# Turning the retention's q and k without TensorE: VectorE squares and transfers, with the row norms broadcast through DRAM and the forget sums made transposed

## The chip, the cores and the metric

The kernel runs on one core of a Trainium2 chip. The metric is device microseconds from launch to end. A core has five engines that matter here, each with its own queue that is worked off in order: TensorE (PE, matrix products), VectorE (DVE), ScalarE (ACT), GpSimd (POOL), and SyncE (SP), which issues nearly all transfers. An instruction that waits holds up everything behind it on its own engine.

## The reference

One decoder block on 512 tokens of width 1024, in float32. Two token mixers run side by side, a chunkwise retention and an attention with forget gates; then come gates, an output projection and a SwiGLU feed-forward part. What the change touches:

```python
q_r = rotary(q_r.reshape(B, S, RET_HEADS, RET_DK), pos)                          # 4 heads of 64
k_r = rotary(k_r.reshape(B, S, RET_HEADS, RET_DK), pos) * (RET_DK ** -0.5)
# retention, chunks of 128 tokens:
scores = jnp.einsum('bnihd,bnjhd->bnhij', qc, kc) * decay[None, None]
intra = jnp.einsum('bnhij,bnjhe->bnihe', scores, vc)
chunk_kv = jnp.einsum('bnjhd,hj,bnjhe->bnhde', kc, zeta, vc)
inter = jnp.einsum('bnihd,bnhde->bnihe', qc, states) * xi[None, None, :, :, None]
# forgetting attention:
log_f = jax.nn.log_sigmoid(f_f.astype(jnp.float32) + b_forget[l].astype(jnp.float32))
c = jnp.cumsum(log_f, axis=1).transpose(0, 2, 1)
s = s + c_blk[..., None] - c[:, :, None, :]
```

`RMSNorm(x)` scales each token by one number (the row norm); the kernel applies it after the product, so for the gates, which are computed with tokens along the free axis, that number must stand in every partition: a [128, 512] tile `r1`.

## The kernel before

Every large product is made in three parts (high x high, low x high, high x low) to keep float32 accuracy. So each weight tile `raw` of 512 KB is loaded by SP, cast by ACT to `wh` (L162) and has its remainder `wl` made by VectorE (L163). There are two `raw` buffers and three pairs of `wh`/`wl`: a load waits until the tile before last has been split, a cast until TensorE is done with the weights three units back.

The stretch in question runs from about 60 to 175 us. TensorE's order there is written out by hand: a generator `fill` yields the weight products of the other projections (for the attention `qf` with 256 and then 264 columns, `kf`, `vf`, and then the gates), and `fill(us)` puts so many microseconds of them between the steps of the retention. The steps work on one chunk t of 128 tokens, t = 0 to 3: `ret_rotate` (POOL, rotary embedding, writes `rot` and the keys `kz`), `ret_turn` (TensorE turns `rot` in four 128 x 128 transposes against an identity, ACT copies them out of a `tp` bank into `rT`, VectorE multiplies the q half by a decay), `ret_scores` (two `tp` banks, products of `rT`, then `kz` x `vr` for the state), `ret_values` (two `sc` banks), `ret_norm` (VectorE, group norm into `og`) and `ret_out` (VectorE gates `og`, TensorE turns it, ACT and VectorE split it into `orh` and `orl`). There are two `tp` banks, so the scores of chunk t+1 need `ret_out` of t-1 to have left its bank: `orl` (L189) is what frees it.

Meanwhile the finished `qf` is squared by ACT, summed and normalized by VectorE (the `n8` instructions, interleaved with the `n4` of the retention's norm) and multiplied by POOL (L642, L644), and then turned through VectorE squares and DRAM (`turn_heads`, `put_heads`, `get_heads`). All transfers after 60 us go through `move` (L72) on SP's one queue, in the order of the program. The function `after(a, b)` only fixes the order of two instructions.

`broadcast_cols` makes `r1`: VectorE spreads the four columns of row norms into `wide`, TensorE turns it (four transposes), ACT copies it out. The forget sums are made as [tokens, heads] by two small products, copied to `cs`, turned by four transposes, and put to DRAM as `cd`.

Of the kernel before, what the change touches and what calls it, by code (L numbers as in the profile page):

```python
# [9 lines left out]
F32 = mybir.dt.float32  # L10
# [42 lines left out]
def block_kernel(ctx: ExitStack, tc, x, xT, c_early, c_tab, c_late, w_qf, w_tok, w_vg, w_a, w_y, w_o, w_gu, w_gl, w_dn, w_dh, out):  # L53
# [198 lines left out]
    ri = sm.tile([P, 32], F32, name="ri", tag="ri", bufs=1)  # L252
    nc.gpsimd.memset(ri, 0.0)

    def broadcast_cols(r, dst, wide=None, behind=None):

        pb = bank("tp")
        if wide is not None:
            one = nc.vector.tensor_copy(out=wide, in_=r.rearrange("p (t o) -> p t o", o=1).broadcast_to([P, NT, P]))
            if behind is not None:  # L260
                after(one, behind)
        for t in range(NT):
            if wide is None:
                rb = sm.tile([P, P], F32, name="rb", tag="rb")
                ts(out=rb, in0=ones, scalar1=r[:, t:t + 1], scalar2=None, op0=ALU.mult)
            turn(pb[:, t * P:(t + 1) * P], rb if wide is None else wide[:, t, :])
        nc.scalar.copy(out=dst, in_=pb)
# [196 lines left out]
    s4 = x_low(0)  # L464
    b6.append(half(B22, 1))
    products(z_, b6, s4, False)
    wide = ftok.tile([P, NT, P], F32, name="wide", tag="sq", bufs=1)
    vr = rtok.tile([P, NT, 512], F32, name="vr", tag="rtok0")
    gs = rtok.tile([P, NT, 512], F32, name="gs", tag="rtok1")
    for v in range(2):  # L470
# [49 lines left out]
    def ret_rotate(t):  # L520
        z5 = rz[:, t, :].rearrange("p (a h s d) -> p a h s d", a=2, h=RH, s=2)
        z1, z2 = z5[:, :, :, 0, :], z5[:, :, :, 1, :]
        c = cosv[:, t].broadcast_to([P, 2, RH, 32])
        s = sinv[:, t].broadcast_to([P, 2, RH, 32])
        rot = rwk.tile([P, 512], F32, name="rot", tag="rot")
        r5 = rot.rearrange("p (a h s d) -> p a h s d", a=2, h=RH, s=2)
        ta = rwk.tile([P, 2, RH, 32], F32, name="ta", tag="ta", bufs=1)
        tb = rwk.tile([P, 2, RH, 32], F32, name="tb", tag="tb", bufs=1)
        first = gp.tensor_tensor(out=ta, in0=z1, in1=c, op=ALU.mult)
        if t == 0:  # L530
            tc.add_manual_dep(first.ins, last_low.ins.name, mybir.DependencyInfo(mybir.DependencyClass.Sync, mybir.DependencyReason.DATA), reason="GpSimd's part comes behind most of the sums")
# [6 lines left out]
        gp.tensor_tensor(out=r5[:, :, :, 1, :], in0=tcc, in1=td, op=ALU.add)
        kz = rwk.tile([P, 256], F32, name="kz", tag="kz")
        last = gp.tensor_tensor(out=kz.rearrange("p (h d) -> p h d", h=RH), in0=rot[:, 256:512].rearrange("p (h d) -> p h d", h=RH),  # L540
                         in1=ce[:, C_ZETA:C_ZETA + RH].rearrange("p (h o) -> p h o", o=1).broadcast_to([P, RH, RDK]), op=ALU.mult)
        ret[t].update(rot=rot, kz=kz, rotated=last)

    def ret_turn(t):
        rot = ret[t]["rot"]
        rT = rwk.tile([P, 6, P], F32, name="rT", tag="rT")
        pt = bank("tp")
        for j in range(4):
            turn(pt[:, j * P:(j + 1) * P], rot[:, j * P:(j + 1) * P])
        nc.scalar.copy(out=rT[:, 0:4, :], in_=pt.rearrange("p (j q) -> p j q", j=4))  # L550
        tt(out=rT[:, 4:6, :], in0=rT[:, 0:2, :], in1=xiT, op=ALU.mult)
        ret[t].update(rT=rT)

    def ret_scores(t):
        rT, kz = ret[t]["rT"], ret[t]["kz"]
        sT = rwk.tile([P, 512], F32, name="sT", tag="sT")
        sps = [bank("tp") for e in range(2)]
        for e, sp in enumerate(sps):
            rows = slice(e * 64, (e + 1) * 64)
            for a in range(2):  # L560
                mm(sp[:, a * P:(a + 1) * P], lhsT=rT[rows, 2 + a, :], rhs=rT[rows, a, :], start=True, stop=True)
            tt(out=sT[:, e * 256:(e + 1) * 256], in0=sp[:, 0:256], in1=dec[:, e * 256:(e + 1) * 256], op=ALU.mult)  # L562
        ret[t].update(sT=sT)
        if t < NT - 1:
            kv = (ret[t - 1]["o"][0] if t else bank("sc"))[:, 256:512]
            for h in range(RH):
                rows = slice((h % 2) * 64, (h % 2 + 1) * 64)
                mm(kv[rows, (h // 2) * P:(h // 2 + 1) * P], lhsT=kz[:, h * RDK:(h + 1) * RDK], rhs=vr[:, t, h * P:(h + 1) * P], start=True, stop=True)
            sn = rwk.tile([P, 2, P], F32, name="sn", tag="sn")
            if t == 0:  # L570
                nc.vector.tensor_copy(out=sn, in_=kv.rearrange("p (a e) -> p a e", a=2))
            else:
                st = ret[t]["st"]
                for a in range(2):
                    stt(out=sn[:, a, :], in0=st[:, a, :], scalar=ce[:, C_GCH + a:C_GCH + a + 1], in1=kv[:, a * P:(a + 1) * P], op0=ALU.mult, op1=ALU.add)
            ret[t + 1].update(st=sn)

    def ret_values(t):
        rT, sT = ret[t]["rT"], ret[t]["sT"]
# [28 lines left out]

    def ret_out(t):
        og = ret[t]["og"]  # L610
        after(gp.tensor_tensor(out=gs[:, t, :], in0=gs[:, t, :], in1=gret, op=ALU.mult), ret[1]["rotated"])
        tt(out=og, in0=og, in1=gs[:, t, :], op=ALU.mult)
# [58 lines left out]
    def turn_heads(z, ts_=range(NT)):  # L671
# [1 line left out]
        if 0 in ts_:  # L673
            turn_heads.sq = rtok.tile([P, 4, 4, NT, 32], F32, name="zsq", tag="rz")
        for t in ts_:
            nc.vector.transpose(out=turn_heads.sq.rearrange("p b a t j -> p a b t j")[:, :, :, t, :], in_=z[:, t, :].rearrange("p (a b j) -> p a b j", a=4, b=4))
# [212 lines left out]
    stt(out=lff, in0=fzf, scalar=0.0, in1=fa, op0=ALU.min, op1=ALU.subtract)
    lp = ftok.tile([P, NT - 1, FH], F32, name="lp")  # L890
    nc.vector.tensor_copy(out=lp[:, 0, :], in_=lf[:, 0, :])
    for j in range(1, NT - 1):
        tt(out=lp[:, j, :], in0=lp[:, j - 1, :], in1=lf[:, j, :], op=ALU.add)
# [12 lines left out]
    pc = bank("tp")
    for t in range(NT):
        turn(pc[0:FH, t * P:(t + 1) * P], cs[:, t, :])
    cT = ftok.tile([FH, S], F32, name="cT", tag="sq", bufs=1)
    nc.vector.tensor_scalar_mul(cT, pc[0:FH, :], -1.0)  # L910
    cd = drp.tile([FH, S], F32, name="cd")
    move(cd, cT)
# [647 lines left out]
```

## Time and profile before

| | |
|---|---|
| median of 3 runs | 683.05 us (683.03 to 683.46) |
| the profiled execution | 682.73 us, its span 680.9 us (1.8 us lie around the span) |
| TensorE busy | 673.2 us, 99% of the span |
| VectorE, ScalarE, GpSimd busy | 535.5, 351.0, 76.2 us |
| granted TensorE clock | 0.999 of full speed |

The profile names engines PE, DVE, ACT, POOL, SP; "PEld" is TensorE's weight load, "SPq" SP's issuing of transfers. A row `tp<-ctab,rot` is an instruction that writes tile `tp` and reads `ctab` (the identity lies in it) and `rot`. Matrix products overlap in the pipeline, so the start of one against the start of the next gives its cost, not its duration. A group in a timeline row ("x4") has one start and one length.

### The profile page before, as it was taken

How to read it: one execution, taken by the hardware profiler on the slowest of the kernel's cores; microseconds unless marked ns; L12 is line 12 of the kernel's file. 1: busy time of each engine (PE TensorE's matmuls, PEld its weight loads, DVE VectorE, ACT ScalarE, POOL GpSimd, SP SyncE). 2: the span in 40 equal slices, each digit the busy share in tenths (PEclk: the TensorE clock that was granted, in tenths of full speed). 3: DMA queues.
4: the chain of work that ended last, by engine and by line, in shares of the span. 5: the costliest groups of instructions: out<-in, count | busy, mean ns of one | idle time of the engine just before them, and what ended most of it. 6: DMA issues, size and time to landing. Idle time of an engine off the chain costs nothing.

```text
span 680.9 us, 9401 instructions
## 1 busy us (share of the span) xinstructions
PE 673.2 (99%) x3399; PEld 564.3 (83%) x3399; DVE 535.5 (79%) x865; ACT 351.0 (52%) x516; POOL 76.2 (11%) x96
## 2 busy tenths in 40 slices
PE   8999999999999999999999999999999999999998
PEld 6888997888886778788888888888888898888998
DVE  6899567777688674596989998989999888556794
ACT  6767452433464445254576655564646474343341
POOL 0013945101122210000130000000000000000000
PEclk9999999999999999999999999999999999999999
DMA  8910312624657886337511516445362513554221
GB/s 277 420 53 32 125 63 61 218 86 163 202 169 217 268 270 208 107 111 278 216 63 49 199 32 191 114 145 153 88 179 59 154 63 81 143 145 159 93 94 63
DMA packets 82223, 98.94 MB, mean 145 GB/s; under 512 B 52472, under 2 KB 59256, under 8 KB 81408
## 3 DMA queue, kind: packets, MB, share of 16 engines
q1 hardware_dynamic: 81392, 97.27, 44.8%
q10 hardware_dynamic: 784, 1.06, 0.6%
q8 instruction: 27, 0.44, 0.3%
q14 instruction: 20, 0.16, 0.1%
HBM read 81.97 MB, written 9.52 MB: 134 GB/s over the span
## 4 chain that ended last, share of the span: by engine, by line
PE 79%; DVE 1%; DMA 1%; issue 1%; ACT 1%; SPq 0%; DVEq 0%; ACTq 0%
PE acc L82 62%; PE sc L82 12%; PE tp L82 5%; DMA pT<-pd 1%; ACT ps L1058 0%; DVE ps L1059 0%; PE tp L85 0%; SPq L72 0%; DVE b L1067 0%; DVE wl L163 0%; DVE psq L751 0%; ACT us L1221 0%; DVE us L1271 0%; DVE orl L189 0%; DVE hl L1115 0%
## 5 line engine op out<-in xcount | busy, mean ns | idle before, releaser
L82 PE MATMUL acc<-ps,xfh 128*128 128x512 f32 (+1 forms) x576 | 166.6, 372 | 0.3 <-ACT us L1180 0.3
L82 PEld LDWEIGHTS acc<-ps,xfh 128*128 128x128 f32 x576 | 105.2, 188 | 19.1 <-ACT us L1180 0.5
L1058 ACT CAST ps<-b 128x1024 fp32r<-128x1024 f32 (+1 forms) x84 | 82.4, 981 | 59.9 <-DVE b L1067 26.7
L1059 DVE TENSOR_TENSOR ps<-b,ps 128x1024 fp32r<-128x1024 f32 (+1 forms) x84 | 94.3, 1135 | 20.1 <-ACT ps L1058 18.9
L82 PE MATMUL acc<-ps,xfl 128*128 128x512 f32 (+1 forms) x288 | 106.9, 371 | 0.0
L162 ACT CAST wh<-raw 128x1024 fp32r<-128x1024 f32 (+1 forms) x44 | 46.0, 1049 | 84.1 <-PE acc L82 42.2
L163 DVE TENSOR_TENSOR wl<-raw,wh 128x1024 fp32r<-128x1024 f32 (+1 forms) x44 | 56.5, 1288 | 24.0 <-ACT wh L162 24.0
L82 PEld LDWEIGHTS acc<-ps,xfl 128*128 128x128 f32 x288 | 54.3, 188 | 9.4
L1067 DVE TENSOR_TENSOR b<-b,b 128x1024 f32<-128x1024 f32 (+1 forms) x48 | 52.1, 1125 | 0.0
L82 PE MATMUL acc<-xh,wh 128*128 128x512 f32 x128 | 50.8, 397 | 0.0
L82 PE MATMUL acc<-wh,xh 128*128 128x512 f32 (+2 forms) x144 | 50.3, 350 | 0.0
L82 PE MATMUL acc<-xl,wh 128*128 128x512 f32 x128 | 50.0, 390 | 0.0
L82 PE MATMUL acc<-xh,wl 128*128 128x512 f32 x128 | 49.9, 390 | 0.0
L82 PE MATMUL acc<-wh,xl 128*128 128x512 f32 (+2 forms) x144 | 49.3, 343 | 0.0
L82 PE MATMUL acc<-wl,xh 128*128 128x512 f32 (+2 forms) x144 | 49.3, 342 | 0.0
L82 PE MATMUL acc<-hl,ps 128*128 128x512 f32 x168 | 40.4, 389 | 0.0
L82 PEld LDWEIGHTS acc<-hl,ps 128*128 128x128 f32 x168 | 31.5, 188 | 6.6
L1180 ACT COPY us<-acc 128x512 f32<-128x512 f32 (+1 forms) x48 | 26.1, 550 | 16.3 <-PE acc L82 15.3
L1106 DVE TENSOR_TENSOR ps<-raw,ps 128x1024 fp32r<-128x1024 f32 x14 | 17.1, 1220 | 18.8 <-ACT ps L1103 18.8
L82 PEld LDWEIGHTS acc<-wh,xh 128*128 128x128 f32 x144 | 27.2, 189 | 3.6 <-DVE sT L562 0.2
L82 PEld LDWEIGHTS acc<-wh,xl 128*128 128x128 f32 x144 | 27.2, 189 | 3.2
L82 PEld LDWEIGHTS acc<-wl,xh 128*128 128x128 f32 x144 | 27.2, 189 | 2.9
(302 smaller groups left out, 1438.8 us busy)
## 6 DMA issues: line engine op xcount, KB each, us to landing
b<-in_w_gu_dram SPq DMA_DIRECT2D x40, 512.0 KB, 4.2
raw<-in_w_a_dram SPq DMA_DIRECT2D x16, 512.0 KB, 4.5
raw<-in_w_dn_dram SPq DMA_DIRECT2D x14, 512.0 KB, 4.0
pd<-psq SPq DMA_DIRECT2D x8, 640.0 KB, 4.5
pT<-pd SPq DMA_DIRECT2D x32, 160.0 KB, 4.5
pf<-squares SPq DMA_DIRECT2D x160, 32.0 KB, 1.9
blk<-in_w_vg_dram SPq DMA_DIRECT2D x8, 512.0 KB, 10.0
raw<-in_w_tok_dram SPq DMA_DIRECT2D x8, 512.0 KB, 3.2
```

Source lines behind the costliest of these rows:

```text
L82: in_order(nc.tensor.matmul(o, **kw))
L162: split_raw.last = (nc.scalar.copy(out=h[:, :width], in_=raw[:, :width]), tt(out=l[:, :width], in0=raw[:, :width], in1=f32(h)[:, :width], ...
L163: tt(out=l[:, :width], in0=raw[:, :width], in1=f32(h)[:, :width], op=ALU.subtract))
L1058: part.cast = nc.scalar.copy(out=h, in_=raw)
L1059: low = tt(out=l, in0=raw, in1=f32(h), op=ALU.subtract)
L1067: queue(tt(out=raws[g][b][v], in0=raws[g][b][v], in1=raws[g][c][v], op=ALU.add))
L1106: tt(out=l, in0=raw, in1=f32(h), op=ALU.subtract)
L1180: copy = nc.scalar.copy(out=u_(tp, slot), in_=os[tp][:, :w])
```

## The change

It has four parts.

- Each chunk's `rot` is turned by one VectorE instruction in 32 x 32 squares (`ret_square`), put to DRAM in four transfers of 64 KB that set the squares in place, and got back as `rT` in one of 256 KB (`ret_get`). ACT copies the k half to `rK` (`ret_keys`), VectorE multiplies the q half into `rX` (`ret_decay`). The 16 transposes and the copies out of `tp` go. `rot` and `kz` get a third buffer, and the rotations are issued one chunk earlier.
- `put_cols` puts the row norms to DRAM, [1, 512], and one transfer reads them back into all partitions as `r1`. The spreading copy, four transposes and a copy go.
- The forget sums are made as [heads, tokens] at once: the log gates are the stationary operand and the triangle and ones move. Four transposes and a copy go.
- Orders: the first step of the log gates (`fa`) and VectorE's turning of `qf` come behind `og` of chunk 0.

```diff
-    def broadcast_cols(r, dst, wide=None, behind=None):
...
+    def put_cols(r, dst):
+
+        move(dst.rearrange("o (t p) -> p (o t)", p=P), r)
...
-    def ret_turn(t):
-        rot = ret[t]["rot"]
-        rT = rwk.tile([P, 6, P], F32, name="rT", tag="rT")
-        pt = bank("tp")
-        for j in range(4):
-            turn(pt[:, j * P:(j + 1) * P], rot[:, j * P:(j + 1) * P])
-        nc.scalar.copy(out=rT[:, 0:4, :], in_=pt.rearrange("p (j q) -> p j q", j=4))
-        tt(out=rT[:, 4:6, :], in0=rT[:, 0:2, :], in1=xiT, op=ALU.mult)
+    def ret_square(t):
+        sq = rwk.tile([P, 4, 4, 32], F32, name="rsq", tag="rsq")
+        one = nc.vector.transpose(out=sq.rearrange("p b a i -> p a b i"), in_=ret[t]["rot"].rearrange("p (a b j) -> p a b j", a=4, b=4))
+        after(one, (turn_of[0], ret[0].get("decay"), ret[1].get("new"), ret[2].get("new"))[t])
+        zd = drp.tile([4, 32, 4, P], F32, name="zr", tag=f"zr{t % 2}")
+        for c in range(4):
+            move(zd[:, :, c, :].rearrange("b j x -> j b x"), sq[32 * c:32 * c + 32].rearrange("p b a i -> p b (a i)"))
+        ret[t].update(zd=zd)
+
+    def ret_get(t):
+        rT = rwk.tile([P, 4, 4, 32], F32, name="rT", tag="rT")
+        move(rT.rearrange("p c a i -> p (c a i)"), ret[t]["zd"].rearrange("b j c x -> (b j) (c x)"))
...
     ret_rotate(0)
+    ret_rotate(1)
+    ret_square(0)
     fill(RF[0])
-    broadcast_cols(rstd1, r1, wide, turn_of[0])
-    ret_turn(0)
-    ret_rotate(1)
+    rd1 = drp.tile([1, S], F32, name="rd1")
+    put_cols(rstd1, rd1)
+    ret_get(0)
+    ret_rotate(2)
     fill(RF[1])
+    move(r1, rd1.broadcast_to([P, S]))
+    ret_keys(0)
     ret_scores(0)
+    ret_decay(0)
+    ret_square(1)
     for t in range(NT):
+        if t == 1:
+            ret_rotate(t + 2)
         fill(RF[2])
         if t + 1 < NT:
-            ret_turn(t + 1)
-            if t + 2 < NT:
-                ret_rotate(t + 2)
+            ret_get(t + 1)
         if t:
             fill(RF[3])
             ret_out(t - 1)
         turn_q()
         fill(RF[3])
+        if t + 2 < NT:
+            ret_square(t + 2)
         turn_q()
+        if t + 1 < NT:
+            ret_decay(t + 1)
+            ret_keys(t + 1)
         ret_values(t)
...
-    mm(cps[:, :NT * FH], lhsT=tri, rhs=lff, start=True, stop=False)
+    mm(cps[rows, :P], lhsT=lf.rearrange("p h t -> p (h t)"), rhs=tri, start=True, stop=False)
```

In the built program SP's queue changes most, where the first weight tiles of this stretch are loaded. `zr` is the DRAM tile of the squares, `rsq` the squares, `r_88` is `r1`:

```order
-L72 DMA raw<-in_w_qf_dram 128x1056 x2
-L72 DMA raw<-in_w_tok_dram 128x1024 x7
+L72 DMA raw<-in_w_qf_dram 128x1056
+L72 DMA zr<-rsq 32x4x128 x4
+L72 DMA raw<-in_w_qf_dram 128x1056
+L72 DMA rd_754<-rstd_86 128x4x1
+L72 DMA rT<-zr 128x512
+L72 DMA r_88<-rd_754 128x512
+L72 DMA zr<-rsq 32x4x128 x4
+L72 DMA raw<-in_w_tok_dram 128x1024 x2
+L72 DMA rT<-zr 128x512
+L72 DMA zr<-rsq 32x4x128 x4
```

Puts and gets of the squares now stand between the weight loads; the first two `w_tok` tiles stand behind the squares of chunk 1.

On VectorE, between the group norm's statistics of chunk 0 (`bs`, `mv`) and the reciprocal roots of the two norms, there now stand the squares of chunk 3 and the decay of chunk 2:

```order
+L604 BN_AGGR mv<-bs 128x2
+L534 STREAM_TRANSPOSE rsq<-rot 128x4x4x32
+L124 TENSOR_SCALAR n8v<-s_651 128x32
 L124 TENSOR_SCALAR n4v<-mv 128x4
+L553 TENSOR_TENSOR rX<-rT,cl 128x256
 L127 TENSOR_SCALAR n8y<-n8v 128x32
```

The two new instructions have come ahead of everything that ends in `og` of chunk 0.

Still on VectorE, in the midst of those roots:

```order
 L132 SCALAR_TENSOR_TENSOR n8y<-n8a,n8y 128x32
 L132 SCALAR_TENSOR_TENSOR n4y<-n4a,n4y 128x4
+L163 TENSOR_TENSOR wl<-raw,wh 128x1024
 L130 SCALAR_TENSOR_TENSOR n8a<-n8y 128x32
 L130 SCALAR_TENSOR_TENSOR n4a<-n4y 128x4
```

One weight remainder has come ahead of `og` of chunk 0; before, it stood behind the turning of `qf`.

And at the end of that chain on VectorE, around `og` itself:

```order
-L606 TENSOR_SCALAR og<-sc,mv,r_1026 128x128 x4
-L551 TENSOR_TENSOR rT<-rT,cl 128x256
-L612 TENSOR_TENSOR og<-og,gs 128x512
-L676 STREAM_TRANSPOSE zsq<-qf 128x4x4x32 x4
-L163 TENSOR_TENSOR wl<-raw,wh 128x1024
+L132 SCALAR_TENSOR_TENSOR r_979<-n8a,n8y 128x32
+L132 SCALAR_TENSOR_TENSOR r_1038<-n4a,n4y 128x4
+L609 TENSOR_SCALAR og<-sc,mv,r_1038 128x128 x4
+L615 TENSOR_TENSOR og<-og,gs 128x512
+L679 STREAM_TRANSPOSE zsq<-qf 128x4x4x32 x3
 L189 TENSOR_TENSOR orl<-tp,orh 128x4x128
```

The decay (`rT`) is gone from between the two `og` instructions, and `orl` comes ahead of the last square and of the remainder.

More of the change, by code (lines that the diff above doesn't have):

```diff
@@ L253, in block_kernel @@
     nc.gpsimd.memset(ri, 0.0)
-    def broadcast_cols(r, dst, wide=None, behind=None):
[L257 to L267, printed above, removed]
+    def put_cols(r, dst):
+        move(dst.rearrange("o (t p) -> p (o t)", p=P), r)
     def tok_group(src, evac, cuts=(512,), done=(), behind=None):
@@ L466, in block_kernel @@
     products(z_, b6, s4, False)
-    wide = ftok.tile([P, NT, P], F32, name="wide", tag="sq", bufs=1)
     vr = rtok.tile([P, NT, 512], F32, name="vr", tag="rtok0")
@@ L524, in ret_rotate @@
         s = sinv[:, t].broadcast_to([P, 2, RH, 32])
-        rot = rwk.tile([P, 512], F32, name="rot", tag="rot")
+        rot = rwk.tile([P, 512], F32, name="rot", tag="rot", bufs=3)
         r5 = rot.rearrange("p (a h s d) -> p a h s d", a=2, h=RH, s=2)
@@ L538, in ret_rotate @@
         gp.tensor_tensor(out=r5[:, :, :, 1, :], in0=tcc, in1=td, op=ALU.add)
-        kz = rwk.tile([P, 256], F32, name="kz", tag="kz")
+        kz = rwk.tile([P, 256], F32, name="kz", tag="kz", bufs=3)
         last = gp.tensor_tensor(out=kz.rearrange("p (h d) -> p h d", h=RH), in0=rot[:, 256:512].rearrange("p (h d) -> p h d", h=RH),
@@ L542, in ret_rotate, with ret_keys, ret_decay @@
         ret[t].update(rot=rot, kz=kz, rotated=last)
-    def ret_turn(t):
-        rot = ret[t]["rot"]
-        rT = rwk.tile([P, 6, P], F32, name="rT", tag="rT")
-        pt = bank("tp")
-        for j in range(4):
-            turn(pt[:, j * P:(j + 1) * P], rot[:, j * P:(j + 1) * P])
-        nc.scalar.copy(out=rT[:, 0:4, :], in_=pt.rearrange("p (j q) -> p j q", j=4))
-        tt(out=rT[:, 4:6, :], in0=rT[:, 0:2, :], in1=xiT, op=ALU.mult)
-        ret[t].update(rT=rT)
+    def ret_square(t):
[9 more added lines that the diff above has]
+        move(rT.rearrange("p c a i -> p (c a i)"), ret[t]["zd"].rearrange("b j c x -> (b j) (c x)"))
+        ret[t].update(rT=rT)
+    def ret_keys(t):
+        rK = rwk.tile([P, 2, P], F32, name="rK", tag="rK")
+        nc.scalar.copy(out=rK.rearrange("p a (c i) -> p a c i", i=32), in_=ret[t]["rT"][:, :, 2:4, :].rearrange("p c a i -> p a c i"))
+        ret[t].update(rK=rK)
+    def ret_decay(t):
+        rX = rwk.tile([P, 2, P], F32, name="rX", tag="rX")
+        ret[t]["decay"] = tt(out=rX.rearrange("p a (c i) -> p a c i", i=32), in0=ret[t]["rT"][:, :, 0:2, :].rearrange("p c a i -> p a c i"),
+           in1=xiT.rearrange("p a (c i) -> p a c i", i=32), op=ALU.mult)
+        ret[t].update(rX=rX)
     def ret_scores(t):
@@ L560, in ret_scores @@
             for a in range(2):
-                mm(sp[:, a * P:(a + 1) * P], lhsT=rT[rows, 2 + a, :], rhs=rT[rows, a, :], start=True, stop=True)
+                mm(sp[:, a * P:(a + 1) * P], lhsT=ret[t]["rK"][rows, a, :], rhs=rT[rows, :, a, :], start=True, stop=True)
             tt(out=sT[:, e * 256:(e + 1) * 256], in0=sp[:, 0:256], in1=dec[:, e * 256:(e + 1) * 256], op=ALU.mult)
@@ L570, in ret_scores @@
             if t == 0:
-                nc.vector.tensor_copy(out=sn, in_=kv.rearrange("p (a e) -> p a e", a=2))
+                new = nc.vector.tensor_copy(out=sn, in_=kv.rearrange("p (a e) -> p a e", a=2))
             else:
@@ L574, in ret_scores @@
                 for a in range(2):
-                    stt(out=sn[:, a, :], in0=st[:, a, :], scalar=ce[:, C_GCH + a:C_GCH + a + 1], in1=kv[:, a * P:(a + 1) * P], op0=ALU.mult, op1=ALU.add)
-            ret[t + 1].update(st=sn)
+                    new = stt(out=sn[:, a, :], in0=st[:, a, :], scalar=ce[:, C_GCH + a:C_GCH + a + 1], in1=kv[:, a * P:(a + 1) * P], op0=ALU.mult, op1=ALU.add)
+            ret[t + 1].update(st=sn, new=new)
     def ret_values(t):
@@ L587, in ret_values @@
                 rows = slice(e * 64, (e + 1) * 64)
-                mm(o[e][:, os], lhsT=rT[rows, 4 + a, :], rhs=ret[t]["st"][rows, a, :], start=False, stop=True, skip_group_check=True)
+                mm(o[e][:, os], lhsT=ret[t]["rX"][rows, a, :], rhs=ret[t]["st"][rows, a, :], start=False, stop=True, skip_group_check=True)
         ret[t].update(o=o)
@@ L610, in ret_out @@
         og = ret[t]["og"]
-        after(gp.tensor_tensor(out=gs[:, t, :], in0=gs[:, t, :], in1=gret, op=ALU.mult), ret[1]["rotated"])
-        tt(out=og, in0=og, in1=gs[:, t, :], op=ALU.mult)
+        after(gp.tensor_tensor(out=gs[:, t, :], in0=gs[:, t, :], in1=gret, op=ALU.mult), ret[2]["rotated"])
+        ret[t]["out"] = tt(out=og, in0=og, in1=gs[:, t, :], op=ALU.mult)
         pt = bank("tp")
@@ L675, in turn_heads @@
         for t in ts_:
-            nc.vector.transpose(out=turn_heads.sq.rearrange("p b a t j -> p a b t j")[:, :, :, t, :], in_=z[:, t, :].rearrange("p (a b j) -> p a b j", a=4, b=4))
+            one = nc.vector.transpose(out=turn_heads.sq.rearrange("p b a t j -> p a b t j")[:, :, :, t, :], in_=z[:, t, :].rearrange("p (a b j) -> p a b j", a=4, b=4))
+            if "out" in ret[0]:
+                after(one, ret[0]["out"])
     def put_heads(z, sq, name):
@@ L883, in block_kernel @@
     fa = ftok.tile([P, NT * FH], F32, name="fa")
-    lf = ftok.tile([P, NT, FH], F32, name="lf")
-    lff = lf.rearrange("p t h -> p (t h)")
-    stt(out=fa, in0=fzf, scalar=-1.0, in1=fzf, op0=ALU.mult, op1=ALU.max)
+    lf = ftok.tile([P, FH, NT], F32, name="lf")
+    lp = ftok.tile([P, FH, NT], F32, name="lp")
+    gp.memset(lp, 0.0)
+    one = stt(out=fa, in0=fzf, scalar=-1.0, in1=fzf, op0=ALU.mult, op1=ALU.max)
+    after(one, ret[0]["out"])
     act(out=fa, in_=fa, func=AF.Exp, scale=-1.0)
     act(out=fa, in_=fa, func=AF.Ln, bias=1.0)
[L889 to L893, printed above, removed]
+    stt(out=lf.rearrange("p h t -> p t h"), in0=fz, scalar=0.0, in1=fa.rearrange("p (t h) -> p t h", t=NT), op0=ALU.min, op1=ALU.subtract)
+    for j in range(NT - 1):
+        tt(out=lp[:, :, j + 1], in0=lp[:, :, j], in1=lf[:, :, j], op=ALU.add)
     put_heads(kf, turn_heads.sq, "k")
@@ L896, in block_kernel @@
     cps = bank("tp")
-    mm(cps[:, :NT * FH], lhsT=tri, rhs=lff, start=True, stop=False)
-    mm(cps[:, FH:NT * FH], lhsT=ones, rhs=lp.rearrange("p t h -> p (t h)"), start=False, stop=True)
-    cs = ftok.tile([P, NT, FH], F32, name="cs")
+    rows = slice(0, FH * NT)
+    mm(cps[rows, :P], lhsT=lf.rearrange("p h t -> p (h t)"), rhs=tri, start=True, stop=False)
+    mm(cps[rows, :P], lhsT=lp.rearrange("p h t -> p (h t)"), rhs=ones, start=False, stop=True)
     ftok.tile([P, PAD_FTOK], F32, name="pad")
-    nc.vector.tensor_copy(out=cs, in_=cps[:, 0:NT * FH].rearrange("p (t h) -> p t h", t=NT))
+    cT = ftok.tile([FH * NT, P], F32, name="cT", tag="sq", bufs=1)
+    nc.vector.tensor_scalar_mul(cT, cps[rows, :P], -1.0)
     get_heads(kf)
@@ L904, in block_kernel @@
     rtok.release()
+    cd = drp.tile([FH, S], F32, name="cd")
+    move(cd.rearrange("h (t q) -> (h t) q", t=NT), cT)
     fill(CF[1])
[L906 to L912, printed above, removed]
     ofp = tc.alloc_tile_pool(name="ofp", bufs=1, side="right")
```

## The prediction

> **What bounds the kernel now.** I read the table of engines first, then TensorE's waits, then the chain that ended last.
>
> ```profile
> PE 673.2 (99%) x3399; PEld 564.3 (83%) x3399; DVE 535.5 (79%) x865; ACT 351.0 (52%) x516; POOL 76.2 (11%) x96
> ```
>
> ```profile
> PE tp L82 <- DVE orl L189: 0.6, 1, 0.6
> ```
>
> ```profile
> 113.74 0.61 DVE orl L189
> ...
> 114.39 0.71 PE tp L82 x4
> ...
> 134.08 0.54 PE tp L82 x8
> ...
> 168.85 0.36 PE tp L82 x4
> ...
> 171.40 0.44 PE tp L85 x4
> ```
>
> TensorE is busy 99% of the span, and in the changed stretch the chain runs over it without a break but for one place: at 114.39 the scores of chunk 2 waited 0.61 us for `orl`, which frees a bank. So an instruction taken from TensorE is time, unless TensorE then waits for something that does not move with it. That is the whole question. The timeline shows the only other gap, and it is at its limit already:
>
> ```profile
> 106.01 0.39 PE L82 MATMUL acc<-wh,xl 128*128 128x512 f32 x1
> 106.38 0.63 PE L85 MATMUL tp<-ctab,og 128*128 128x128 f32 x4
> ```
>
> A product of 512 columns costs 0.23 us (from start to start), so TensorE was ready at 106.24 and began to turn `og` of chunk 0 at 106.38. VectorE ended that `og` at 104.47 + 1.77 = 106.24:
>
> ```profile
> 92.13 0.59 DVE L655 SCALAR_TENSOR_TENSOR fz<-acc,rstd,ce 128x8 f32<-128x8 f32 x2 [2.36 <-ACT qf L653]
> 93.01 0.69 DVE L636 TENSOR_REDUCE s<-sq 128x8 f32<-128x512 f32 x1 [0.29 <-ACT sq L635]
> ...
> 97.55 1.21 DVE L163 TENSOR_TENSOR wl<-raw,wh 128x1024 fp32r<-128x1024 f32 x1
> ...
> 102.19 1.36 DVE L606 TENSOR_SCALAR og<-sc,mv,r 128x128 f32<-128x128 f32 x4
> 103.47 1.07 DVE L551 TENSOR_TENSOR rT<-rT,cl 128x256 f32<-128x256 f32 x1
> 104.47 1.77 DVE L612 TENSOR_TENSOR og<-og,gs 128x512 f32<-128x512 f32 x1
> 106.16 0.70 DVE L676 STREAM_TRANSPOSE zsq<-qf 128x512 f32<-128x512 f32 x1
> ```
>
> From 92.13 to 106.24, 14.1 us, VectorE has one gap of 0.29 us. It is the bound of this short stretch beside TensorE, and TensorE arrives exactly when it is done.
>
> **What goes from TensorE.**
>
> ```profile
> L85 PE MATMUL tp<-ctab,rot x16: 271/272/273, 73.5 to 122.2; 128*128 128x128 f32 x16
> L85 PE MATMUL tp<-ctab,wide x4: 272/272/273, 73.1 to 73.4; 128*128 128x128 f32 x4
> L85 PE MATMUL tp<-ctab,cs x4: 272/272/273, 171.2 to 171.6; 128*8 128x128 f32 x4
> ```
>
> 24 transposes go. Four stand in the chain for 0.44 us (171.40), so this is 6 x 0.44 = 2.64 us. The forget sums stay four instructions: 0.36 us before (168.85); with 128 columns moving they cost between 4/8 of the scores' 0.54 = 0.27 and a transpose's 0.44, so nothing is charged. The scores now read `rT` as four runs of 32 columns; I charge nothing, with an end of +0.2 us: the retention's scores of all chunks are 32 instructions at 0.07, and a tenth more is 0.2. With both waits gone as well, 2.64 + 0.61 + 0.14 = 3.4 us is the ceiling.
>
> **The first chunk: puts and a get before the scores.**
>
> ```profile
> 65.48 1.06 POOL L538 TENSOR_TENSOR rot<-tcc,td 128x256 f32<-128x256 f32 x1
> ```
>
> ```profile
> L72 SPq DMA_DIRECT2D zd<-zsq x8: 423/576/1558, 115.9 to 152.6; - x8
> ```
>
> ```profile
> pf<-squares SPq DMA_DIRECT2D x160, 32.0 KB, 1.9
> ...
> raw<-in_w_qf_dram SPq DMA_DIRECT2D x2, 528.0 KB, 3.5
> ...
> zd<-zsq SPq DMA_DIRECT2D x8, 256.0 KB, 4.8
> cb<-cd SPq DMA_DIRECT2D x8, 256.0 KB, 4.4
> ...
> b<-in_w_gl_dram SPq DMA_DIRECT2D x8, 256.0 KB, 3.0
> ```
>
> ```profile
> 71.89 0.33 SPq L72 DMA_DIRECT2D raw<-in_w_qf_dram  x1
> ```
>
> ```profile
> 75.55 1.08 ACT L162 CAST wh<-raw 128x1056 fp32r<-128x1056 f32 x1 [0.73 <-DMA raw<-in_w_qf_dram]
> ...
> 78.12 1.57 ACT L653 ACTIVATE qf<-acc,rstd 128x256 f32<-128x256 f32 x4 [1.50 <-PE acc L82]
> ```
>
> ```profile
> 79.00 0.29 PE L82 MATMUL acc<-wh,xh 128*128 128x264 f32 x1
> ```
>
> `rot` of chunk 0 is done at 66.5. VectorE's square takes the place of the spreading copy at 67.1 and its 0.70 us, so 67.8. Four puts take SP 4 x 0.42 = 1.7 to 4 x 0.78 = 3.1 us; I take 2.8, since each has as many rows as the `zd` puts, but a quarter of the bytes. A put of 64 KB lands in 1.9 to 4.8 us, nearest to the 32 KB row. The load of 71.89 then goes out as before; behind it the put of the row norms (0.6 us of issue, an estimate from the smallest of these) and the get of `rT` at about 73.2. The get lands 3.0 (`b`, same size) to 4.4 us (`cb`) later; with the load in front of it I take 3.8: 77.0. Before the scores, TensorE needs its first 264-column product at 79.00 - 0.88 = 78.1, for which ACT must have copied out a bank (0.4 us), and that copy now stands behind `rK` (0.5 us). So `rT` is free up to 77.1. It costs nothing at 77.0, 1.3 us at 78.4.
>
> **The second chunk, SP's queue and where VectorE's chain starts.**
>
> ```profile
> 76.66 2.13 DVE L163 TENSOR_TENSOR wl<-raw,wh 128x1056 fp32r<-128x1056 f32 x1 [0.83 <-ACT wh L162]
> ```
>
> ```profile
> 73.60 0.33 SPq L72 DMA_DIRECT2D raw<-in_w_tok_dram  x1
> ```
>
> ```profile
> 94.74 0.50 PE L82 MATMUL acc<-wh,xh 128*128 128x512 f32 x1
> ```
>
> ```profile
> L551 DVE TENSOR_TENSOR rT<-rT,cl x4: 416/906/1069, 74.8 to 125.3; 128x256 f32<-128x256 f32 x4
> ```
>
> The squares of chunk 1 stand behind that remainder (78.8) and the decay (0.9): 80.4. Their puts hold SP until 83.2, and only then come the two `w_tok` loads, the first of which went out at 73.60. They land at about 86.7 and 88.2 (3.5 us, and 1.5 for the second 512 KB), the second is cast by 89.2, `rT` of chunk 1 lands behind them at 89.1, the decay ends at 90.0, the remainder at 91.2. TensorE needs these weights from 94.74 - 1.32 = 93.4 and, 24 products later, from 98.9: hidden. But `fz`, which could start at 92.13 - 1.32 = 90.8, starts at 91.2. VectorE's idle 2.36 us ahead of it were the cover, and they are used up.
>
> **The chain to `og`.** Its 14.1 us lose the gap (0.3) and the decay between the `og` instructions (1.0), and gain the squares of chunk 3 (0.7), the decay of chunk 2 (0.45) and a weight remainder (1.15): 15.1 us. So `og` is done at 91.2 + 15.1 = 106.3 and TensorE resumes at 106.4. TensorE itself, 16 transposes lighter, is there at 106.24 - 1.76 = 104.5. It waits 1.9 us, and the 1.76 us are gone again.
>
> The price of the last product is open: it took 1.77 us where the others took 0.69.
>
> ```profile
> L612 DVE TENSOR_TENSOR og<-og,gs x4: 679/692/1772, 104.5 to 158.6; 128x512 f32<-128x512 f32 x4
> ```
>
> ```profile
> 102.22 2.04 POOL L642 TENSOR_TENSOR qf<-qf,r 128x512 f32<-128x512 f32 x2 [6.64 <-ACT wh L162]
> ```
>
> The slow one ran beside POOL's product of `qf`, which starts with the same reciprocal root as `og`; after the change it does so again, so I take 1.77 and keep 0.69 as the lower end. [...]
>
> **After that.**
>
> ```profile
> 110.67 0.71 DVE L676 STREAM_TRANSPOSE zsq<-qf 128x512 f32<-128x512 f32 x1 [2.54 <-POOL qf L644]
> ...
> 123.82 0.68 DVE L612 TENSOR_TENSOR og<-og,gs 128x512 f32<-128x512 f32 x1
> ```
>
> ```profile
> 127.28 0.44 PE tp L85 x4
> ```
>
> `orl` stood behind the fourth square and a remainder, ending at 114.34; now it stands behind the third square, which waits for POOL. POOL starts when the roots are done, 1.1 us later (91.2 + 10.1 - 0.3 + 2.3 = 103.3 against 102.2), so the square ends at 110.67 + 1.1 + 0.7 = 112.5, `orl` at 113.2; TensorE needs it at 113.8. The wait of 0.61 is gone. The rest falls where VectorE has slack (`og` of chunk 1 was done 2.8 us ahead of TensorE): 8 transposes, 0.88 us. Later chunks' puts and gets have over 10 us of cover.
>
> **The sum.** At `og` 0.0; wait for `orl` -0.6; last 8 transposes -0.9: -1.5 us. On the profiled 682.73 (0.05% under the median) this is 681.2; on the median 683.05 it is 681.5. A measurement of this kernel tells about 0.2%, 1.4 us, from no change: that lies just inside "faster".
>
> **Rivals.**
>
> *The full gain.* `fz` starts at 90.8 and the last product takes 0.69: `og` at 90.8 + 14.0 = 104.8, TensorE resumes at 104.9 (-1.5); with -0.6 and -0.9, 680.1. For it: TensorE is 99% busy, and a VectorE that finds its inputs ready may close up. Against: 2.3 us of new work in a chain that had 0.3 us of air.
>
> *No difference.* Each transfer takes its longer row: `rT` of chunk 1 lands near 91, `fz` starts at 93.0, `og` ends at 108.1. Then +1.8 at `og`, -0.6, -0.9: 683.3. For it: the two loads and the get share SP's queue. Against: the transfer engines were little used there.
>
> *Slower: `rT` of chunk 0 lands late.* TensorE's bank copy waits behind `rK` on ACT, and VectorE's chain moves with TensorE. If L is the landing, `fz` starts at 90.8 + (L - 77.1) and `og` ends 15.1 later, so the time is 683.05 + L - 79.0: slower from 79.0 on, measurably from 80.4. Puts that land in 4.8 us (last one out at 69.8), a get at 74.7 and 6 us for it (behind a 3.5 us load and hundreds of four-byte rows of the row norms) give 80.7, so 684.8. For it: three dependent steps through DRAM within 10 us. Against: the small puts of 1.9 us.
>
> **How the numbers follow.** Forecast 0.50 (its own range 680.8 to 682.5; three fifths of it under 681.7), full gain 0.20, no difference 0.15, slower 0.15. So faster 0.30 + 0.20 = 0.50, same 0.20 + 0.15 = 0.35, slower 0.15. The range runs from the full gain to just short of the slower rival: 680.0 to 684.3.
>
> **What would show it.** No transposes of `rot`, `wide`, `cs`; TensorE's wait for `orl` gone, and a new wait of 1 to 2 us in front of the transposes of `og` of chunk 0; `fz` near 91.2; `rT` of chunk 0 read by ACT near 77; the first `w_tok` load about 10 us later than 73.60. Wrong would be: a wait at the first 264-column product (the slower rival), or none at `og` (the full gain), or a wait for weights around 95.

## The result and the profile after

| | before | after |
|---|---|---|
| time, median (range of 5) | 683.05 us (682.43 to 683.69) | 689.02 us (688.31 to 689.96) |
| span of the profiled execution | 680.9 us | 686.8 us |

After over before is 1.0088, 95% interval 1.0073 to 1.0103: 6 us slower. The forecast was 681.5. TensorE lost the 24 transposes, and yet it is busy for 1.0 us more than before (674.2 against 673.2), a share of 98% instead of 99%. The table of engines and TensorE's waits, changed kernel:

```profile
PE 674.2 (98%) x3375; PEld 562.7 (82%) x3375; DVE 534.9 (78%) x867; ACT 349.8 (51%) x515; POOL 74.3 (11%) x97
```

```profile
PE acc L82 <- ACT qf L656: 3.6, 1, 3.6
PE tp L85 <- DVE og L615: 1.5, 2, 0.8
...
PE tp L85 <- PE acc L82: 1.0, 1, 1.0
```

The columns are the total, the count and the longest. The wait for `orl` is gone, as forecast. New are 3.6 us in one piece, and three waits ahead of the transposes of `og` (1.0 for chunk 0, 1.5 for chunks 1 and 2). The profile puts the wait of chunk 0 down to a product (`acc`), in later views to "issue"; but in each of these runs VectorE ended that `og` 0.1 us before TensorE went on (111.58 and 111.68 here), so it is `og` that is waited for. The chain that ended last shows what the first one hangs on:

```profile
72.82 0.43 SPq L72
...
73.43 8.33 DMA rT<-zr
...
81.78 0.41 ACT rK L548
82.19 0.38 ACT qf L656
82.57 0.04 issue
82.62 0.63 PE acc L82 x3
```

SP issues the put of the row norms at 72.82 and the get of `rT` of chunk 0 at 73.43. The get takes 8.33 us, ScalarE copies its keys to `rK`, only then comes the bank copy `qf`, and TensorE's first 264-column product starts at 82.62 instead of 79.00. The DMA list (size in KB, median us from issue to landing) and SP's timeline of the changed kernel:

```profile
rT<-zr SPq DMA_DIRECT2D x4, 256.0 KB, 4.1
...
rd<-rstd SPq DMA_DIRECT2D x1, 2.0 KB, 8.8
```

```profile
81.61 0.32 SPq L72 DMA_DIRECT2D r<-rd  x1
83.09 1.80 SPq L72 DMA_DIRECT2D zr<-rsq  x4
```

The other gets of `rT` take about 4 us. The put of 2 KB takes 8.8 us (the get of `r1`, which SP holds back for it, goes out at 81.61), and the get of `rT` behind it lands at 81.76, 0.2 us after the put.

The wait has a tail. The next view gives, for each stretch of the changed kernel, TensorE's busy time, the granted clock, the DMA share and GB/s:

```profile
80.00:82.00 2.00, 0.00 (x0) 1.00 0.00 0
82.00:84.00 2.00, 1.38 (x15) 1.00 0.46 42
84.00:86.00 2.00, 2.00 (x14) 0.55 0.89 216
86.00:88.00 2.00, 2.00 (x13) 0.60 1.01 289
88.00:90.00 2.00, 2.00 (x19) 1.00 0.85 325
```

For some 3.4 us products start 0.22 us apart instead of 0.12. Lined up instruction by instruction, the two kernels stand 3.62 us apart at the first 264-column product and 5.23 us at 87.60: the clock costs another 1.6 us.

### The profile page after: what moved, and what is told of

It reads as the page before. It is cut to its first block, busy times and chain, and to the rows that moved or that the text cites. A ratio compares the mean times of both kernels' runs of the same rounds, so it can differ in the third digit from the quotient of the medians.

```text
span 686.8 us, 9389 instructions
## 1 busy us (share of the span) xinstructions
PE 674.2 (98%) x3375; PEld 562.7 (82%) x3375; DVE 534.9 (78%) x867; ACT 349.8 (51%) x515; POOL 74.3 (11%) x97
## 4 chain that ended last, share of the span: by engine, by line
PE 74%; DVE 10%; DMA 6%; issue 4%; ACT 4%; POOL 2%; SPq 0%; DVEq 0%; ACTq 0%; POOLq 0%
PE acc L82 57%; PE sc L82 12%; PE tp L82 4%; DVE wl L163 2%; DMA pd<-psq 1%; DMA rT<-zr 1%; DMA raw<-in_w_tok_dram 1%; ACT wh L162 1%; DMA cb<-cd 1%; POOL qf L647 1%; DVE pr L742 1%; DMA tk<-tk 1%; DVE ps L1072 1%; POOL qf L645 1%; DMA pT<-pd 1%
## 5 line engine op out<-in xcount | busy, mean ns | idle before, releaser
L162 ACT CAST wh<-raw 128x1024 fp32r<-128x1024 f32 (+1 forms) x44 | 46.1, 1050 | 81.6 <-PE acc L82 45.3
L1193 ACT COPY us<-acc 128x512 f32<-128x512 f32 (+1 forms) x48 | 26.1, 551 | 16.0 <-PE acc L82 15.1
```

The lines of the kernel that those rows point to most:

```text
L162: split_raw.last = (nc.scalar.copy(out=h[:, :width], in_=raw[:, :width]), tt(out=l[:, :width], in0=raw[:, :width], in1=f32(h)[:, :width], ...
L1193: copy = nc.scalar.copy(out=u_(tp, slot), in_=os[tp][:, :w])
```

## Experiments

All ratios are to runs of the kernel before on the same chip, with 95% intervals. The kernel before itself ran from 682.3 to 686.9 us there, so ratios are compared, not times.

### Where the put of the row norms stands

**e1**: put and get of `r1` moved behind the last get of `rT`.

```diff
-    rd1 = drp.tile([1, S], F32, name="rd1")
-    put_cols(rstd1, rd1)
     ret_get(0)
...
-    move(r1, rd1.broadcast_to([P, S]))
...
             ret_get(t + 1)
+        if t + 1 == NT - 1:
+            rd1 = drp.tile([1, S], F32, name="rd1")
+            put_cols(rstd1, rd1)
+            move(r1, rd1.broadcast_to([P, S]))
```

> The changed kernel, with the put of the row norms and the get of r1 moved behind the get of rT of the last chunk; nothing else is edited. Theory A (the put of 512 four-byte elements, landing after 8.8 us, holds the get of rT of chunk 0 behind it in SP's queue): the get lands about 4 us after its issue instead of 8.3, TensorE's 3.6 us wait at the first 264-column product shrinks to under 0.6 us, the granted clock stays at 1.0 between 84 and 88 us, and the time falls by 3.6 + 1.65 us to about 683.8 us (682.8 to 684.8). Theory B (a get through DRAM that follows its puts so closely is late by itself): the first get still takes about 8 us, the wait stays at 3 us or more, and the time stays at 688 to 689 us.

Measured: 1.0002 (0.9990 to 1.0015). The put is as slow as ever (9.2 us), but the get of `rT`, issued at 72.12, lets ScalarE go on at 77.18, TensorE does not wait at that product, and the clock stays at 1.00. The first row is from ScalarE's timeline of e1, the second from TensorE's:

```profile
77.18 0.41 ACT L548 COPY rK<-rT 128x256 f32<-128x256 f32 x1 [0.70 <-DMA rT<-zr]
```

```profile
78.02 0.39 PE L82 MATMUL acc<-wh,xh 128*128 128x264 f32 x1
```

Theory A holds; nearly the whole 6 us are the place in the queue of this one put and of the get of `r1` that waits for it. e11 and e12 take the two apart.

**e2**: the put stays in its place, but writes 128 rows of 16 bytes instead of 512 single values.

```diff
-        move(dst.rearrange("o (t p) -> p (o t)", p=P), r)
+        move(dst.rearrange("o (p t) -> p (o t)", p=P), r)
```

(The gates then read `r1` as "p (q t) -> p t q".)

> The changed kernel with the row norms laid out in DRAM as 128 rows of four contiguous values (16 bytes) instead of 512 single values; the put stands at the same place in SP's queue, and the gates read r1 through a permuted view. Theory A, by the number of elements: the put lands in 2 to 4 us, the get of rT of chunk 0 in 4 to 5, TensorE's wait falls to about 0.5 us and the time to about 684 us (683 to 685). Theory C (any put in front of the get costs its whole round trip, whatever its elements): the put still lands after 7 us or more and the time stays above 688 us.

Measured: 1.0008 (0.9995 to 1.0020).

```profile
rd<-rstd SPq DMA_DIRECT2D x1, 2.0 KB, 4.6
```

The same 2 KB in a quarter of the pieces land in 4.6 us, and the get behind them at about 77.7. So it is the pieces, neither the bytes nor the round trip as such; whether their number or their size counts, e2 does not separate, since it changes both.

**e11 and e12**: the changed kernel with the get of `rT` ahead of the put (e11), and besides with the get of `r1` moved to the place it has in e1 (e12).

```diff
+    ret_get(0)
     rd1 = drp.tile([1, S], F32, name="rd1")
     put_cols(rstd1, rd1)
-    ret_get(0)
```

> The changed kernel with two lines exchanged: the get of rT of chunk 0 is issued ahead of the put of the row norms instead of behind it; the get of r1 stays where it was. Theory A (what stands behind the put in SP's queue is late, first the get of rT, then everything behind the get of r1, for which SP itself waits): rT of chunk 0 lands 4 to 5 us after its issue and TensorE's wait at the first 264-column product falls under 0.6 us. But SP stands still until about 82 us as before, the squares of chunk 1 go out near 83 us and rT of chunk 1 lands near 91 us; fz starts about 2 us later than in e1, TensorE's wait for og of chunk 0 grows from 1.85 to about 3.9 us, and above 2 us of idling the granted clock falls and costs some 1.5 us more: ratio 1.002 to 1.006, between e1 (1.0002) and the changed kernel (1.0088). Theory B (the first get through DRAM is late by itself): 1.008 to 1.009.

Measured: 1.0059 (1.0036 to 1.0081). The first get now lands in time, but SP stands at the get of `r1` until 83.89, the puts of chunk 1's squares go out at 84.25, and its `rT` at 89.30. The bill comes later, and not quite where I expected it (at `og`): TensorE waits for `fz`, which stands on VectorE behind the decay of chunk 2, and that waits for its get (TensorE's waits and VectorE's timeline of e11):

```profile
PE acc L82 <- DVE fz L658: 3.0, 1, 3.0
```

```profile
98.54 0.43 DVE L553 TENSOR_TENSOR rX<-rT,cl 128x256 f32<-128x256 f32 x1 [3.38 <-DMA rT<-zr]
```

> The kernel of e11_swapped with the get of r1 moved behind the get of rT of the last chunk, so that SP does not wait for the put's landing; the put itself stays at about 73 us, behind the get of rT of chunk 0. Theory A with the SP wait as the second cost: everything goes as in e1, ratio 1.0002 (0.999 to 1.001). Rival: what is issued while the put is under way (puts of the squares of chunk 1, from 78.5 us) is held as the get was, and lands only when the put has landed, near 82 us: rT of chunk 1 and fz come up to 2 us later, ratio 1.001 to 1.004.

Measured: 1.0025 (1.0013 to 1.0037): the rival, though the interval just touches that of e1. SP issues the squares of chunk 1 at 78.66 and the get of their `rT` only at 85.62; in e1 these are 78.52 and 81.69. The weight load issued right behind the squares reaches ScalarE at 87.51, in e1 at 84.37. This trace has no landing for the put; issued at 73.46, it would land at 82.3 to 85.3 by the 8.8 to 11.8 us of the other runs, so that it was still under way is inferred. SP's waits between 78 and 92 us in e12, and then in e1:

```profile
SPq L72 <- DMA zr<-rsq: 4.1, 1, 4.1
```

```profile
SPq L72 <- DMA zr<-rsq: 0.3, 1, 0.3
```

TensorE waits 2.22 us at `og` of chunk 0 instead of 1.85, and its clock falls (0.50 from 109 to 111 us). So in these runs the put holds both ways: SP itself, where an instruction waits for its landing (in e11 the put goes out at 74.08 and SP's next transfer at 83.89), and what is issued behind it (SP's 4.1 us at the squares here, 0.3 in e1; that the put was still under way is inferred).

### What the drop of the clock costs

**e3**: 14 products of 512 columns with unused results ahead of the first 264-column product of the changed kernel.

```diff
+            if w == 264:
+                spin = bank("tp")
+                for _ in range(14):
+                    mm(spin, lhsT=xh[:, 0, 0:P], rhs=xh[:, 0, :], start=True, stop=True)
```

> The changed kernel with 14 extra products of 512 columns (3.2 us, results not used) on TensorE directly ahead of the first 264-column product, inside the 3.6 us in which it waits there. Theory A (after the idle stretch the granted clock falls to 0.5 to 0.7 for about 3 us and costs 1.65 us): the clock stays at 1.0 through 84 to 88 us, the 264-column products start 0.12 us apart at once, and the time falls to about 687.4 us (686.9 to 687.9). Rival: the clock drop costs nothing at the end, since later waits of TensorE for og take it up: 689.0 us.

Measured: 1.0104 (1.0082 to 1.0126), no gain. The put took 10.3 us in the profiled execution, TensorE still idled 1.99 us, and there the clock stayed up. But `og` of chunk 0 depends on VectorE, which was late by the landing, so TensorE then waited there 2.39 us and the clock fell at that place (timeline and stretch of e3):

```profile
84.13 0.39 PE L82 MATMUL acc<-wh,xh 128*128 128x264 f32 x1 [1.99 <-ACT qf L660]
...
113.09 0.63 PE L85 MATMUL tp<-ctab,og 128*128 128x128 f32 x4 [2.39 <-issue]
```

```profile
114.00:116.00 2.00, 2.00 (x6) 0.50 0.00 0
```

The edit also shifted a few instructions of chunk 2 on ScalarE and VectorE. The total effect of the clock is thus not isolated; its local price is read from the traces, below.

### The forget sums alone

**e4**: the kernel before with only the part of the change on the forget sums, and the log-gate chain `fa` left where it was.

```diff
-    mm(cps[:, :NT * FH], lhsT=tri, rhs=lff, start=True, stop=False)
...
+    mm(cps[rows, :P], lhsT=lf.rearrange("p h t -> p (h t)"), rhs=tri, start=True, stop=False)
...
-        turn(pc[0:FH, t * P:(t + 1) * P], cs[:, t, :])
```

> The kernel before with only the forget sums made transposed (four transposes fewer, one copy fewer, the put of the sums earlier); the retention and the row norms stay as they were. If TensorE's instructions are what counts there: 0.4 us faster, 682.6 us. Rival: the chain of small VectorE steps ahead of the sums or the new layout costs as much as it saves: 683.1 us, or up to 0.5 us slower.

Measured: 1.0024 (1.0011 to 1.0036), slower. At the values of the first pair of heads TensorE waits 1.91 us for a get of `pT` where it waited 1.27 before, so what was saved ahead of that is lost there (timeline of e4):

```profile
215.88 2.37 PE L82 MATMUL tp<-pT,vf 128*64 128x512 f32 x14 [1.91 <-DMA pT<-pd]
```

That explains why there is no gain. The remaining loss is not explained: at the second pair TensorE loses another 1.3 us in this profiled execution, for which the profile names no releaser, and e1, which holds the same edit, loses 0.45 there. It stays open.

### What is left: three waits for `og`

In e1 TensorE waits for `og` of chunks 0, 1 and 2 (timeline of e1):

```profile
106.43 0.63 PE L85 MATMUL tp<-ctab,og 128*128 128x128 f32 x4 [1.85 <-issue]
...
126.56 0.63 PE L85 MATMUL tp<-ctab,og 128*128 128x128 f32 x4 [0.80 <-DVE og L615]
...
145.89 0.63 PE L85 MATMUL tp<-ctab,og 128*128 128x128 f32 x4 [0.69 <-DVE og L615]
```

For chunk 1, VectorE's timeline (e1) has this ahead of the group norm:

```profile
115.00 0.18 DVE L905 SCALAR_TENSOR_TENSOR fa<-fz 128x32 f32<-128x32 f32 x1
117.02 0.22 DVE L909 SCALAR_TENSOR_TENSOR lf<-fz,fa 128x32 f32<-128x32 f32 x1 [1.84 <-ACT fa L908]
```

The change put `fa` behind `og` of chunk 0. Before, `fa` ran at 99.36 and `lf` found it ready at 115.39; now VectorE stands still for ScalarE's Exp and Ln.

**e5**: e1 with the log-gate chain behind `og` of chunk 2.

```diff
-    after(one, ret[0]["out"])
+    after(one, ret[2]["out"])
     act(out=fa, in_=fa, func=AF.Exp, scale=-1.0)
```

> The kernel of e1_norms_late (row norms put behind the last get of rT) with one more edit: the log-gate chain fa (VectorE, then Exp and Ln on ScalarE, then lf and lp) is ordered behind og of chunk 2 instead of behind og of chunk 0, so VectorE no longer sits 1.84 us at lf ahead of chunk 1's group norm. Theory A (that wait made og of chunk 1 late): TensorE's wait at og of chunk 1, 0.80 us in e1, is gone, and the time is 0.8 us under e1, ratio to before 0.9990. Rival (waits in series: TensorE arriving earlier finds og of chunk 2 late instead, 0.69 us in e1): the wait there grows by 0.8 us and the ratio stays at 1.0002.

Measured: 0.9970 (0.9959 to 0.9980), faster than both kernels. The waits at `og` of chunks 1 and 2 are both gone:

```profile
108.07 0.63 PE L85 MATMUL tp<-ctab,og 128*128 128x128 f32 x4 [1.84 <-issue]
...
127.23 0.60 PE L85 MATMUL tp<-ctab,og 128*128 128x128 f32 x4
...
145.67 0.60 PE L85 MATMUL tp<-ctab,og 128*128 128x128 f32 x4
```

That is 2.2 us by the ratios where I expected 0.8; the second wait moved with the first.

**e6, e7, e8**: three attempts at `og` of chunk 0.

```diff
-        after(one, (turn_of[0], ret[0].get("decay"), ret[1].get("new"), ret[2].get("new"))[t])
+        after(one, (turn_of[0], ret[0].get("decay"), ret[1].get("new"), ret[0].get("out"))[t])
...
+        if t > 1:
+            after(ret[t]["decay"], ret[t - 2]["out"])
```

> The kernel of e1_norms_late with the decay of chunk 2 and the square of chunk 3 ordered behind og of chunk 0 on VectorE (they stood ahead of it: 0.60 us, 1.24 us of waiting for the get of rT, and 0.68 us). Theory A (VectorE's chain to og of chunk 0 holds TensorE for 1.85 us): og comes 1.3 to 2.5 us earlier, the wait there falls under 0.6 us and the time falls by 1.3 to 1.85 us, ratio 0.9973 to 0.9983. Rival (waits in series): the work moved behind og makes og of chunk 1 later by what TensorE gained, its wait grows from 0.8 to about 2.5 us, and the ratio stays at 1.0002.

> Both edits of e5 and e6 together, and the squares of the forget keys ordered behind og of chunk 2 (the first of them waits 1.21 us for GpSimd ahead of that chunk's group norm). Theory A (three waits of TensorE for og, 1.85 + 0.80 + 0.69 us, are all that is left of the 3.4 us ceiling): all three shrink under 0.5 us, and the time is 2.4 to 3.3 us under e1, ratio 0.9954 to 0.9967, about 680.3 us. Rival: another wait takes their place (orl of chunk 0, which stands here behind all four squares of q, 0.6 us, or the put of the keys' squares): ratio 0.998 to 1.000.

> The kernel of e7_all_late with the third and fourth square of q ordered behind orl of chunk 0. Theory A: TensorE's wait for orl of chunk 0 (0.6 us in the kernel before) does not come back, and the time is 0 to 0.6 us under e7, ratio 0.9945 to 0.9965. Rival: the later squares of q delay their puts, and the forget part starts later by as much: the same as e7 or slower.

Measured: 1.0107 (1.0094 to 1.0120), 1.0139 (1.0126 to 1.0152) and 1.0062 (1.0048 to 1.0076): none as expected. The wait at `og` of chunk 0 did go in each, but the square of chunk 3 came late, and its puts stand in SP's queue ahead of the row norms. SP's and ScalarE's timelines of e6:

```profile
113.28 1.78 SPq L72 DMA_DIRECT2D zr<-rsq  x4
...
116.85 0.43 SPq L72 DMA_DIRECT2D rd<-rstd  x1
127.61 0.32 SPq L72 DMA_DIRECT2D r<-rd  x1
128.03 0.38 SPq L72 DMA_DIRECT2D raw<-in_w_tok_dram  x1
```

```profile
134.11 1.04 ACT L162 CAST wh<-raw 128x1024 fp32r<-128x1024 f32 x1 [8.37 <-DMA raw<-in_w_tok_dram]
```

SP stands 10.8 us for the landing of the 2 KB, the weight load behind it goes out at 128.03 (116.80 in e5), ScalarE waits 8.37 us for it and TensorE 5.6 us. In e7 and e8 the same load goes out at 129.31 and 127.27. By these traces it is the same put that made the changed kernel slow, at another place.

**e9 and e10**: e5 with the decay of chunk 2 alone behind `og` of chunk 0 (e9), and besides with the 16-byte rows of e2 (e10).

```diff
+        if t == 2:
+            after(ret[t]["decay"], ret[0]["out"])
         ret[t].update(rX=rX)
```

> The kernel of e5_gate_late with the decay of chunk 2 alone ordered behind og of chunk 0 (it stood ahead of it and waited 1.15 us for the get of rT, then took 0.70 us); the square of chunk 3 stays where it was. Theory A (what made e6 slow was the late square: its puts held SP's queue, the put of the row norms behind them landed at 127.6 us and the weight load behind that came 7 to 8 us late; the decay itself is harmless): og of chunk 0 comes 1.75 us earlier, TensorE's wait there falls from 1.8 to about 0.1 us, and the ratio falls from 0.9970 to about 0.9945 (0.994 to 0.9955). Rival (the decay moved behind og is what made e6 slow, or og of chunk 1 takes the gain): ratio 0.9965 or more.

> The kernel of e9_gate_decay_late with the row norms put as 128 rows of 16 bytes. Theory A: the get of r1 waits 4 to 5 us instead of 10 to 11 behind its put, SP's queue is free again by about 110 us, but nothing there is late in e9 either, so the time is that of e9 (within 0.1%). Rival: the 11 us in which SP's queue stands still cost something in e9 as well (weight loads or the puts of q's squares go out late): 0.2% or more under e9.

Measured: 0.9959 (0.9946 to 0.9972) and 0.9958 (0.9944 to 0.9972). The wait at `og` of chunk 0 fell from 1.84 to 0.74 us in both, not to 0.1; the step from 0.9970 is in the expected direction, but within the intervals. So the decay was harmless, and the late square was what broke e6. That it did so through the put behind it is read from the trace of e6; no run has the late square with the 16-byte rows. The 16-byte rows change nothing where nothing waits. By the ratios either kernel is 0.4% faster than the kernel before, and 1.3% than the changed one.

## Why the prediction was wrong

**The first chunk.** This is the step that failed: "behind it the put of the row norms (0.6 us of issue, an estimate from the smallest of these) and the get of `rT` at about 73.2. ... with the load in front of it I take 3.8: 77.0". The issue was right (0.43 us, get at 73.43). What I priced was the put's time on SP; its time to land, which the get behind it shares, was left out. The get took 8.3 us. Without the put ahead of it, it took 5.0 (e1), and 3.8 and 4.1 with the put behind it (e11, e12); TensorE felt none of these. That e1's get landed at 77.16, so near the forecast 77.0, is luck: it was issued 1.1 us earlier than forecast and took 1.2 us longer. The trace of before has no put under 16 KB, and of those one kind lands in 2.2 us and another (`rd<-rt`) in 5.7, which should have warned me; I bounded the get by loads of 256 KB instead.

The slower rival named the place ("hundreds of four-byte rows of the row norms") and its rule was 683.05 + L - 79.0. With the measured L of 81.76 it gives 685.8. The other 3.2 us of the 689.0 are about what the rule leaves out: 1.6 us of granted clock after the wait, and the waits for `og` of chunks 1 and 2 (1.5 us).

**The transposes.** 24 fewer. TensorE in e1 is 0.93 us ahead of the kernel before at 73.9 and 1.70 us ahead at 101.4, by 8 and 16 transposes; the forecast had 0.88 and 1.76. Right, though 0.14 us of it was there before the first transpose in these two executions.

**The second chunk, the chain to `og`, and its wait.** With the put out of the way (e1) TensorE resumed at `og` of chunk 0 at 106.43 after 1.85 us of waiting; the forecast was 106.4 and 1.9. `fz` started at 90.78 (forecast 91.2), and the chain took 15.5 us (15.1). The terms were less exact than the sum: the last product took 1.21 us instead of 1.77, the decay of chunk 2 cost 0.60 plus 1.24 us of waiting for its get, where I had 0.45, and some of the others took less. On the last product my reading was off: before, the GpSimd product beside it was neither of the two of L642 that I showed (the second ended at 104.26, ahead of the start at 104.47) but the next, of L644, 1.47 us long. In both kernels `og` ended 0.55 us after the GpSimd product that was under way at its start (105.69 and 106.24 before, 111.03 and 111.58 in the changed kernel). So in these two executions what it lost against the 0.69 us of the others (1.08 and 0.53 us) went with what that product still had to run (1.22 and 0.67 us), and was no fixed price. What couples the two engines no run shows. In the changed kernel itself the chain ran from 96.91 to 111.58, and the wait was 0.97 us, since TensorE was late as well.

**After that.** The wait for `orl` is gone, as forecast. "The rest falls where VectorE has slack" was the second step to fail. I priced the transposed forget sums on TensorE only, and gave no price to the order that puts `fa` behind `og` of chunk 0, though it stands in the list of the change: VectorE then waits for ScalarE's answer ahead of the next group norm. It cost the two waits, 1.5 us, as much as the whole forecast gain: e1 came out at 1.0002, and e5, with `fa` out of the way, 2.0 us under the kernel before.

So by the ratios, 5.9 of the 6 us go with the place of the put and of the get that waits for it (each ratio is known to about 0.0013, 0.9 us). The two profiled executions, of the changed kernel and of e1, lie 5.3 us apart: 3.75 us come in at the wait, 1.5 with the clock, and there are 0.85 by which the changed kernel's was behind before the wait began, less the 0.9 that TensorE then waits less at `og` of chunk 0.

## What to carry over

A small transfer is not priced by its bytes or its issue (2 KB and 0.43 us of issue here, 8.8 us to land): ask how many separate pieces it writes, when it lands, and what stands behind it in its queue or waits for it on the issuing engine. Put such a transfer where nothing urgent follows (e1: 1.0002 for 1.0088), or give it longer rows (e2: 4.6 us to land, 1.0008). Whether issuing it from another engine's queue would do as well was not tried. And when an edit reorders an instruction "on the side", list what it waits for and which chain stands behind it on that engine; two of the three surprises here, the put on SP's queue (8.33 us for the get behind it) and `fa` on VectorE's (1.84 us of standing still), were in-order queues, not work.

## What the hardware showed that I had not expected

**A put that holds its queue.** 2 KB in 512 four-byte pieces landed after 8.8 to 11.8 us in the nine runs that show it, in 128 pieces after 4.6 (e2) and 3.6 (e10). The get issued behind it on the same queue finished no earlier than it did (81.8 against 81.6 in the changed kernel, 83.3 against 83.1 in e3, 77.7 against 77.3 in e2). In the changed kernel the get of `rT` was complete 0.2 us after the put, though the transfer engines had been nearly idle since 78 us (DMA share 0.03 from 78 to 80 us, 0.00 from 80 to 82). What makes the get wait for the put no run shows. Standing just ahead of the put was not always safe either: the last get of `rT`, issued 0.4 us before it, took 8.2 us in e1 and 8.8 in e9, but 2.8 to 5.4 in e5 to e8, as did the first one in e11 and e12. Why is open; TensorE did not wait for it in either.

**The clock can fall after little more than 2 us of idling.** In the profiled executions, TensorE's waits of 1.84 (e5), 1.85 (e1), 1.91 (e4) and 1.99 us (e3) left the granted clock at 1.00. Waits of 2.22 (e12), 2.39 (e3), 2.57 (e7), 3.02 (e11) and 3.61 us (after) brought it to 0.50 for 3.4 us, and those of 3.18 (e7), 5.59 (e6) and 5.91 us (e8) for 6.8. The timeline and a stretch of e12:

```profile
107.75 0.76 PE L85 MATMUL tp<-ctab,og 128*128 128x128 f32 x4 [2.22 <-issue]
108.16 0.78 PE L82 MATMUL acc<-wh,xh 128*128 128x512 f32 x1
...
109.59 0.63 PE L82 MATMUL acc<-wh,xh 128*128 128x512 f32 x1
```

```profile
109.00:111.00 2.00, 2.00 (x6) 0.50 0.01 3
```

In the changed kernel and in e12 the drop cost 1.5 to 1.6 us, by the shift of the instructions behind it.

In these executions a wait of 2.2 us was thus worth nearly 4 us, one of 1.9 us only itself. The limit is not sharp: one drop of 3.4 us brings the mean clock of a run to about 0.9975 (0.5 x 3.4 of 684 us), and of twelve runs each, eight of e12 but also three of e1 have a mean of 0.997 or 0.998. How long TensorE waited in the runs without a profile is not on record.
